# The compressed unit of a prompt's attention: four-pass float32 product, or one float32r product of split operands

## The chip, the cores and the metric

The kernel runs on one core of a Trainium2 chip. The metric is the device time of one execution in microseconds; the median of several runs is compared. Times inside an execution come from one profiled execution, in microseconds (us) from the start of its span. PE is TensorE's stream of matrix products, PEld its loads of weights, DVE VectorE, ACT ScalarE, POOL GpSimd and SP SyncE.

## What is computed

One step of a one-layer decoder trunk, for a prompt of 1024 positions and for eight samples of eight positions: half a SwiGLU, a mixer of attention (8 query heads of 64, 2 key/value heads) and Mamba-2, another half SwiGLU, a last norm. The attention has three branches, whose outputs are weighted by gates and added. The change concerns the first of them, in the prompt: keys and values summarised from blocks of 32 positions at a stride of 16, so 63 rows for 1024 positions. Cut to it, the reference is:

```python
def compress(rows, pe, w1, w2):
    ...   # blocks of 32 rows, stride 16, plus pe
    return jax.nn.silu(blk @ w1) @ w2

def cmp_attention(q, q_pos, kc, vc, slopes):
    ...
    s = jnp.einsum('btghd,bngd->bghtn', qg, kc).astype(jnp.float32) / math.sqrt(HEAD_DIM)
    ...
    p = masked_softmax(s, dist >= 0)
    o = jnp.einsum('bghtn,bngd->btghd', p.astype(vc.dtype), vc)
    return o.reshape(b, Tq, ATT_HEADS, HEAD_DIM), p

o = g[:, :, 0] * o_cmp + g[:, :, 1] * o_sel + g[:, :, 2] * o_win
```

All is float32.

## The kernel before

The kernel goes through its stages in the order of the text: first feed-forward, projections and state-space mixer, keys and values, queries, the prompt's attention, the samples' attention with the output projection, second feed-forward, last norm. Within a stage, and some way across its borders, the order of instructions on each engine is made at build time by a scheduler that works with estimated durations and priorities; on the chip each engine then goes through its own queue in that order, and semaphores hold an instruction until its operands are there.

**Two kinds of products.** Most products of the kernel are done in float32r after a split of each operand into a high part (rounded to float32r, usually by ScalarE) and a low part (the rest, by a subtraction): `split(hi, lo, src, eng)`. The products of probabilities with values are done in plain float32 instead, and show as two records each in the trace.

**Values.** In the stage of keys and values, `cmp_finish(1, ab)` makes the 63 summarised value rows of both groups in one PSUM tile `c2p` (L1523) and copies them into `VAc`, 64 rows by 2 groups by 64 columns, in the pool `kv`, zeroed by GpSimd at L1404 (the 64th row stays zero). `VA` holds the full value rows of the two other branches by blocks of 128 positions. `KA`, the keys, lies behind `VAc` in the pool.

**The prompt's attention** (from L1752) runs over eight tiles of 128 queries in the order 2, 7, 6, 5, 4, 3, 1, 0. Between them it also summarises the samples' cached rows (`compress_sample`: rows gathered into `chk`, products `cA`, L1733 to L1735), so that these products lie in the same stretch of TensorE's queue. For a tile the scores of all heads with the summarised keys are made (`s_cmp`), turned into probabilities `pc` and scaled by the gate. Then for each of the two groups of four heads: scores `s` with the keys of the two other branches (L1808, L1810, masks L1813), their maxima (L1818, L1821, L1822), exponentials `pb` (L1824), scaling by the gate, and a loop over the "units". A unit is one block of 128 key positions, or, as the last one, the 64 compressed rows. For each unit four transposes (L1846) put the probabilities of the four heads side by side into one PSUM tile `pT` (two of them), a copy brings it to `pt` (VectorE or ScalarE in turn), and a product (L1855) of weights `VA` or `VAc` and moving `pt` adds to the PSUM tile `O`. Units go in pairs: an even unit writes rows 0 to 63 of `O`, an odd one rows 64 to 127, issued one behind the other. The number of full units is 2, 4, 6, 8, 10, 11, 12, 13 for tiles 0 to 7; so the compressed unit stands alone but in tiles 5 and 7, where it is the second of a pair. At the end of a group the upper half of `O` is copied to `ob` and added to the lower half into `qT` (L1865, L1866). `O` is one PSUM tile, used by all groups in turn.

Of the functions below, the lines that matter are `VAc` at L1401, L1404 and L1526, and the loop over units from L1838 to L1859.

Of the kernel before, what the change touches and what calls it, by code (L numbers as in the profile page):

```python
# [10 lines left out]
F32 = mybir.dt.float32  # L11
F32R = mybir.dt.float32r
# [6 lines left out]
P = 128  # L19
# [22 lines left out]
def f32(ap):  # L42
    return ap.bitcast(F32)
# [37 lines left out]
def hybrid_step(ctx: ExitStack, tc: tile.TileContext, *aps):  # L81
    nc = tc.nc
# [4 lines left out]
    def pool(name, bufs=1, side="left", space=None, reuse="tile"):  # L87
        kw = {} if space is None else {"space": space}
        if space is None:
            kw["side"] = side  # L90
        return tc.tile_pool(name=name, bufs=bufs, reuse_waits=reuse, **kw)
# [101 lines left out]
    def side(name):  # L193
        return PS.tile([P, 512], F32, name=name, tag="side", bufs=3)
# [71 lines left out]
    def copy(eng, out, src):  # L266
        return nc.scalar.copy(out, src) if eng == "a" else ENGINES[eng].tensor_copy(out, src)  # L267

    def sub(eng, out, x, y, op=OP.subtract):
        ENGINES[eng].tensor_tensor(out, x, y, op=op)  # L270
# [10 lines left out]
    def split(hi, lo, src, eng, heng="a"):  # L281
        copy(heng, hi, src)
        sub(eng, lo, src, f32(hi))
# [380 lines left out]
    K = F1  # L664
# [728 lines left out]
    KV = KVs.enter_context(pool("kv"))  # L1393
# [4 lines left out]
    VA = KV.tile([P, 2, 8, 2, 64], F32, name="VA")  # L1398
    KAc = KV.tile([P, 2, 64], F32R, name="KAc")
    KBc = KV.tile([P, 2, 64], F32R, name="KBc")  # L1400
    VAc = KV.tile([64, 2, 64], F32, name="VAc")  # L1401
    KA = KV.tile([P, 2, 2, TP], F32R, name="KA")
    for t_ in (f32(KAc), f32(KBc), VAc):
        nc.gpsimd.memset(t_, 0.0)  # L1404

    def cmp_hidden(K, ya, yb, kv, m, bufs=1):

        xh = K.tile([P, 2, 2, m + 1], F32, name="cxh", tag="nat", bufs=bufs)
        x_, hs = xh[:, 0], xh[:, 1]
        nc.scalar.activation(x_[:, :, :m], ya, AF.Identity, bias=biask[:, kv:kv + 1])  # L1410
        if yb is not None:
            nc.vector.tensor_tensor(x_[:, :, :m], x_[:, :, :m], yb, op=OP.add)
        nc.scalar.activation(hs[:, :, :m], x_[:, :, :m], AF.Tanh, scale=0.5)
        nc.vector.scalar_tensor_tensor(hs[:, :, :m], hs[:, :, :m], 1.0, x_[:, :, :m], op0=OP.add, op1=OP.mult)
        return hs

    with pool("kvt", bufs=2) as KT, pool("kvtmp", bufs=2) as K:
# [93 lines left out]
        def cmp_finish(kv, ab):  # L1511
            va, vb = (x[:, :P].rearrange("p (g c) -> p g c", g=2) for x in ab)
            hs = cmp_hidden(K, va[:, :, :63], vb[:, :, 1:], kv, 63, 2)
            q = side("c2p")
            if kv == 0:
                kc = q[:64, :126].rearrange("p (g n) -> p g n", g=2)
                nc.tensor.matmul(kc, w2[:, 0], hs[:, :, :63], start=True, stop=True)
                nc.scalar.copy(KAc[0:64, :, :63], kc)
                nc.vector.tensor_copy(KBc[0:64, :, :63], f32(KAc[0:64, :, :63]))
                nc.vector.tensor_tensor(KAc[64:128, :, :63], kc, f32(KAc[0:64, :, :63]), op=OP.subtract)  # L1520
            else:
                for g in range(2):
                    nc.tensor.matmul(q[:63, 64 * g:64 * g + 64], hs[:, g, :63], w2[:, 1],  # L1523
                                     start=True, stop=True)
                vc = q[:63, :P].rearrange("p (g d) -> p g d", g=2)
                nc.vector.tensor_copy(VAc[:63], vc)  # L1526

        def keys(br, kT):
            a = br - 1
# [26 lines left out]
        for c in range(3, 5):  # L1556
            gate(G, hs[:, c - 3], c)
        cmp_finish(0, ab)
        ab = cmp_products(1, *rows_)
        keys(1, k1)  # L1560
# [6 lines left out]
        hs = G.tile([P, 3, 2, P], F32, name="hs", bufs=1)  # L1567
        gate(G, hs[:, 0], 6)
        cmp_finish(1, ab)
        positions(0)  # L1570
        v2 = proj(2, 1)
# [102 lines left out]
    with pool("att", bufs=2) as K, pool("att_ps2", bufs=3, space=PSUM) as PS2, \  # L1674
            pool("att_ps", bufs=1, space=PSUM) as PS1:
        def b1(name):
            tag = "cT" if name == "c2" else name
            return PS1.tile([P, 512], F32, name=name, tag=tag, bufs=2 if name == "pT" else 1)
# [72 lines left out]
        for qi, qt in enumerate(KN["qt"]):  # L1751
# [13 lines left out]
            for h in range(NH):  # L1765
# [5 lines left out]
                             start=False, stop=True, skip_group_check=True)  # L1771
# [13 lines left out]
            for g in range(2):  # L1785
                PT = {}
                for br in range(2):
# [6 lines left out]
                    for hh_ in range(4):  # L1794
                        pb = K.tile([P, 1024 if br == 0 else 640], F32, name=f"pb{br}", bufs=5)
                        pbs.append(pb)
                        st, parts = 0, []
                        for i in range(ns):
# [7 lines left out]
                            if br == 1 and qt >= 4 and st == 0:  # L1806
                                masks.append((0, medge))
                            nc.tensor.matmul(s, QAs[g][:, hh_], KA[:, br, g, kk], start=True, stop=False,  # L1808
                                             skip_group_check=True)
                            nc.tensor.matmul(s, QBq[g][:97, hh_], KB[:97, br, g, kk], start=False, stop=not masks,  # L1810
                                             skip_group_check=True)
                            for j, (c, mk) in enumerate(masks):
                                nc.tensor.matmul(s[:, c:c + P], identb, mk, start=False,  # L1813
                                                 stop=(j == len(masks) - 1), skip_group_check=True)
# [18 lines left out]
                    for hh_ in range(4):  # L1833
                        h, pb = 4 * g + hh_, pbs[hh_]
                        scale(KN["pb"][qi][4 * br + hh_], pb[:, :nk], pb[:, :nk], sm[:, 1 + br, h:h + 1])
                    PT[br] = (pbs, k0, nk // P)
                O = b1("o")
                units = [(VA[:, br, PT[br][1] + i, g], PT[br][0], i, P)  # L1838
                         for br in range(2) for i in range(PT[br][2])]
                units.append((VAc[:, g], None, 0, 64))  # L1840
                held = []
                for ui, (v, pb, i, kn) in enumerate(units):
                    tq_ = b1("pT")
                    for hh_ in range(4):
                        src = pb[hh_][:, P * i:P * i + P] if pb is not None else pc[:, 4 * g + hh_, :]
                        nc.tensor.transpose(tq_[:kn, P * hh_:P * hh_ + P], src, ident)  # L1846

                    pt = K.tile([P, 512], F32, name="pt", bufs=4)
                    c_ = copy("av"[ui % 2], pt[:kn], tq_[:kn])
                    held.append((v, pt[:kn]))  # L1850
                    if ui % 2 or ui == len(units) - 1:

                        with tc.high_priority():
                            for u, (v_, p_) in enumerate(held):
                                mm = nc.tensor.matmul(O[64 * u:64 * u + 64], v_, p_, start=(ui < 2), skip_group_check=True,  # L1855
                                                      stop=(ui - len(held) + 1 + u >= len(units) - 2))
                                if u < len(held) - 1:
                                    tc.add_manual_dep(mm.ins, c_.ins.name, mybir.DependencyInfo(
                                        mybir.DependencyClass.Sync, mybir.DependencyReason.DATA), reason="pair")  # L1859
                        held = []  # L1860
# [470 lines left out]
    for j, m in enumerate(MB[5:] + MB[:5]):  # L2331
# [13 lines left out]
        for i, n in blocks(288):  # L2345
            nc.tensor.matmul(sums[:n, i:i + 1], sq[:, P * i:P * i + n], ones[:, :1], start=(j == 0 and i == 0),
                             stop=(j == KD - 1), skip_group_check=True)
# [185 lines left out]
```

## Time and profile before

| | before |
|---|---|
| runs, us | 2471.36, 2468.21, 2470.27 (median 2470.27) |
| profiled execution, us | 2475.45 |
| its span, us | 2473.8 |
| keys, values, queries | to 1138 us |
| prompt's attention | 1138 to 1550 us |
| samples' attention and output projection | 1550 to about 1760 us |
| TensorE busy, share of the span | 97% |

The shares of busy time on the page are averages over all stages. The windows cut them by stage. The chain of work follows the end of the run, or of a stretch, back through what released each instruction; time on it is time that the end waited for. In a timeline the start of an instruction and that of the next on the same engine give what it holds the engine; a record of TensorE is longer than that, since the ends of its instructions overlap the next ones.

### The profile page before, as it was taken

What the parts mean: (1) busy time and instruction counts of PE and PEld (TensorE: products, weight loads), DVE (VectorE), ACT (ScalarE), POOL (GpSimd) and SP (SyncE); (2) the same over time, 40 slices, a digit from 0 to 9 for tenths busy, and PEclk for the clock granted to TensorE, in tenths of its full rate; (3) what the DMA queues carried; (4) which work ended last, traced back from release to release, by engine and by line L of the source; (5) the groups of instructions that cost most, each with busy time, mean ns of one, the idle gap of its engine ahead of it and who ended that gap; (6) DMA issues with size and microseconds to landing.
All of it is one profiled execution on the core that took longest, in us unless ns stands there. A gap on an engine that the chain in (4) does not pass through costs nothing.

```text
span 2473.8 us, 48193 instructions
## 1 busy us (share of the span) xinstructions
PE 2408.8 (97%) x19026; PEld 2222.8 (90%) x19026; DVE 1744.7 (71%) x3673; ACT 1131.2 (46%) x2501; POOL 418.3 (17%) x533
## 2 busy tenths in 40 slices
PE   7999999999999999999999999999999999999998
PEld 6999999999999998997667766677899999999998
DVE  6777776677778855655656666777967676768776
ACT  7544444441133254425666675444545454543113
POOL 0000000011134343333434343111000000001110
PEclk9999999999999999999999998999999999999999
DMA  4334343598652333423110104476235353559654
GB/s 162 134 133 160 130 164 129 175 338 306 230 190 84 126 116 102 119 69 127 40 64 35 69 35 148 130 250 213 89 123 171 120 174 120 174 213 370 238 209 153
DMA packets 230446, 379.07 MB, mean 153 GB/s; under 512 B 18509, under 2 KB 147705, under 8 KB 228812
## 3 DMA queue, kind: packets, MB, share of 16 engines
q1 hardware_dynamic: 210248, 318.02, 37.7%
q0 software_dynamic: 7600, 38.59, 4.5%
q10 hardware_dynamic: 12372, 19.38, 2.2%
q8 instruction: 150, 2.46, 0.4%
q14 instruction: 76, 0.62, 0.1%
HBM read 255.66 MB, written 124.40 MB: 154 GB/s over the span
## 4 chain that ended last, share of the span: by engine, by line
PE 86%; DVE 6%; DMA 4%; ACT 3%; issue 1%; POOL 0%; ACTq 0%; DVEq 0%; POOLq 0%
PE dq L634 6%; PE gY L367 6%; PE dq L633 6%; PE dq L635 6%; PE gY L368 6%; PE gY L366 6%; PE gX L367 5%; PE gX L366 5%; PE gX L368 5%; PE o L1855 3%; PE pT L1846 3%; PE s L1808 1%; PE xbc L250 1%; PE xbc L251 1%; PE xbc L252 1%; PE cA L1733 1%
## 5 line engine op out<-in xcount | busy, mean ns | idle before, releaser
L634 PE MATMUL dq<-db,da 128*128 128x256 f32 (+1 forms) x1232 | 353.2, 288 | 0.3 <-DVE da L270 0.3
L635 PE MATMUL dq<-db,da 128*128 128x256 f32 (+1 forms) x1232 | 352.8, 288 | 0.0
L633 PE MATMUL dq<-db,da 128*128 128x256 f32 (+1 forms) x1232 | 349.8, 288 | 2.7 <-DVE Cc L386 2.2
L642 DVE TENSOR_TENSOR xT<-xT,dq 128x256 f32<-128x256 f32 (+1 forms) x456 | 186.9, 432 | 84.8 <-PE dq L635 83.2
L270 POOL TENSOR_TENSOR ds<-dw 128x512 f32<-128x512 f32 x22 | 29.5, 1341 | 1228.1 <-DVE wlo L270 508.0
L633 PEld LDWEIGHTS dq<-db,da 128*128 128x128 f32 x1232 | 230.5, 189 | 3.3 <-DVE Cc L386 2.5
L635 PEld LDWEIGHTS dq<-db,da 128*128 128x128 f32 x1232 | 232.8, 189 | 0.0
L634 PEld LDWEIGHTS dq<-db,da 128*128 128x128 f32 x1232 | 231.9, 188 | 0.6 <-DVE da L270 0.5
L267 ACT CAST whi<-ws 128x512 fp32r<-128x512 f32 x156 | 96.5, 623 | 205.9 <-PE gY L368 137.6
L270 DVE TENSOR_TENSOR wlo<-raw,whi 128x512 fp32r<-128x512 f32 x184 | 125.5, 687 | 83.9 <-ACT whi L267 83.5
L267 ACT CAST da<-ds 128x512 fp32r<-128x512 f32 x88 | 52.6, 623 | 234.7 <-PE dq L635 93.4
L267 ACT CAST whi<-raw 128x512 fp32r<-128x512 f32 x181 | 112.4, 626 | 72.0 <-PE g L414 19.5
L270 DVE TENSOR_TENSOR wlo<-ws,whi 128x512 fp32r<-128x512 f32 x156 | 106.7, 687 | 42.4 <-ACT whi L267 41.9
L1824 ACT ACTIVATE pb<-s,mx 128x256 f32<-128x256 f32 (+3 forms) x192 | 105.0, 552 | 59.7 <-DVE mx L1822 37.6
L1846 PEld LDWEIGHTS pT<-ident,pb 128*128 128x128 f32 x528 | 59.6, 143 | 45.8 <-issue 40.1
L1821 DVE TENSOR_REDUCE mx<-s 128x1 f32<-128x384 f32 (+2 forms) x128 | 66.6, 536 | 44.0 <-PE s L1813 34.1
L366 PE MATMUL gY<-B3h,whi 128*128 128x256 f32 (+1 forms) x320 | 91.5, 287 | 1.5 <-ACT whi L267 1.4
L366 PE MATMUL gX<-B6h,whi 128*128 128x256 f32 (+1 forms) x320 | 91.3, 286 | 0.9 <-ACT Cc L373 0.9
L367 PE MATMUL gX<-B6h,wlo 128*128 128x256 f32 (+1 forms) x320 | 91.4, 286 | 0.6 <-DVE wlo L270 0.6
L367 PE MATMUL gY<-B3h,wlo 128*128 128x256 f32 (+1 forms) x320 | 91.6, 287 | 0.2 <-DVE wlo L270 0.2
L277 POOL TENSOR_TENSOR pb<-pb,sm 128x640 f32<-128x640 f32 (+7 forms) x70 | 85.1, 1238 | 37.6 <-DVE sm L1831 34.0
L367 PE MATMUL gY<-B2h,wlo 128*128 128x256 f32 (+1 forms) x320 | 91.4, 286 | 0.0
(763 smaller groups left out, 8548.1 us busy)
## 6 DMA issues: line engine op xcount, KB each, us to landing
db<-GD SPq DMA_DIRECT2D x42, 1632.0 KB
GD<-Cc SPq DMA_DIRECT2D x154, 272.0 KB
GD<-his SPq DMA_DIRECT2D x84, 272.0 KB
raw<-in_ffn_wu_dram SPq DMA_DIRECT2D x22, 1024.0 KB
dw<-in_ffn_wd_dram SPq DMA_DIRECT2D x44, 512.0 KB
raw<-in_ffn_wg_dram SPq DMA_DIRECT2D x21, 1024.0 KB
GD<-hp SPq DMA_DIRECT2D x70, 272.0 KB
db<-GD SPq DMA_DIRECT2D x14, 1088.0 KB
```

Source lines behind the costliest of these rows:

```text
L267: return nc.scalar.copy(out, src) if eng == "a" else ENGINES[eng].tensor_copy(out, src)
L270: ENGINES[eng].tensor_tensor(out, x, y, op=op)
L277: nc.gpsimd.tensor_tensor(out, x, by.to_broadcast(list(x.shape)), op=OP.mult)
L366: nc.tensor.matmul(q, ah[:, k], b_, start=first, stop=False, skip_group_check=True)
L367: nc.tensor.matmul(q, al[:, k], b_, start=False, stop=False, skip_group_check=True)
L368: nc.tensor.matmul(q, ah[:, k], c_, start=False, stop=(k == 3), skip_group_check=True)
L633: nc.tensor.matmul(q, x, bh[:, u, o], start=first, stop=False, skip_group_check=True)
L634: nc.tensor.matmul(q, y, bh[:, u, o], start=False, stop=False, skip_group_check=True)
L635: nc.tensor.matmul(q, x, bl[:, u, o], start=False, stop=(u == np_ - 1), skip_group_check=True)
L642: nc.vector.tensor_tensor(x, x, q, op=OP.subtract if i == 4 else OP.add)
L1824: nc.scalar.activation(pb[:, st:st + pn], s, AF.Exp, bias=mx[:, 0:1], accum_out=part[:, hh_, i:i + 1])
L1846: nc.tensor.transpose(tq_[:kn, P * hh_:P * hh_ + P], src, ident)
```

## The change

`VAc` becomes 128 rows by 2 groups by 128 columns of float32r: the high parts of the values in columns 0 to 63, the low parts in 64 to 127, and the same 64 rows once more in rows 64 to 127 (a copy of rows 0 to 62 to 64 to 126). For the compressed unit the transposed probabilities are split: the high parts go to rows 0 to 63 of a float32r tile `ph`, the low parts to rows 64 to 127. `ph` takes its place among the four buffers of `pt`. One product of 128 rows, 128 columns of weights and 512 moving columns then writes all 128 rows of `O`: rows 0 to 63 get the high values with both parts of the probabilities, rows 64 to 127 the low values with both, and the two halves are added at the end of the group as before. The compressed unit takes no part in the pairs any more. A last full unit with an even number (tiles 5 and 7) is issued alone.

```diff
-    VAc = KV.tile([64, 2, 64], F32, name="VAc")
+    VAc = KV.tile([P, 2, P], F32R, name="VAc")
     KA = KV.tile([P, 2, 2, TP], F32R, name="KA")
-    for t_ in (f32(KAc), f32(KBc), VAc):
+    for t_ in (f32(KAc), f32(KBc), f32(VAc)):
         nc.gpsimd.memset(t_, 0.0)
...
-                nc.vector.tensor_copy(VAc[:63], vc)
+                split(VAc[:63, :, :64], VAc[:63, :, 64:], vc, "v")
+                nc.vector.tensor_copy(VAc[64:127], f32(VAc[:63]))
...
+                    if pb is None:
+                        ph = K.tile([P, 512], F32R, name="ph", tag="pt", bufs=4)
+                        split(ph[:64], ph[64:], tq_[:64], "v")
+                        with tc.high_priority():
+                            nc.tensor.matmul(O, v, ph, start=False, stop=True, skip_group_check=True)
+                        continue
                     pt = K.tile([P, 512], F32, name="pt", bufs=4)
-                    c_ = copy("av"[ui % 2], pt[:kn], tq_[:kn])
-                    held.append((v, pt[:kn]))
-                    if ui % 2 or ui == len(units) - 1:
+                    c_ = copy("av"[ui % 2], pt, tq_)
+                    held.append((v, pt))
+                    if ui % 2 or ui == len(units) - 2:
...
-                                                      stop=(ui - len(held) + 1 + u >= len(units) - 2))
+                                                      stop=False)
```

## Rows read from the trace of the kernel before

**Rows 1.** The page: busy time (us, share, instructions), and its chain by engine.

```profile
PE 2408.8 (97%) x19026; PEld 2222.8 (90%) x19026; DVE 1744.7 (71%) x3673; ACT 1131.2 (46%) x2501; POOL 418.3 (17%) x533
...
PE 86%; DVE 6%; DMA 4%; ACT 3%; issue 1%; POOL 0%; ACTq 0%; DVEq 0%; POOLq 0%
```

**Rows 2.** Windows: us; busy of PE, PEld, DVE, ACT, POOL; granted clock; DMA.

```profile
1060.00:1138.00 78.00, 77.24 (x620) 76.11 (x619) 41.25 (x99) 20.86 (x35) 27.81 (x62) 1.00 0.31 101
1138.00:1550.00 412.00, 398.86 (x2651) 285.98 (x2651) 265.17 (x641) 267.73 (x721) 159.31 (x235) 0.98 0.19 68
```

**Rows 3.** The chain of work from 1138 to 1550 us, shares by line.

```profile
by line: PE o L1855 19.1%; PE pT L1846 15.8%; PE s L1808 7.9%; PE cA L1733 6.9%; PE cA L1735 6.5%; PE s L1810 6.3%; PE cA L1734 6.3%; PE cT L1712 6.3%; DMA chk<-in_cache_cmp_dram,idx 4.8%; PE s L1813 2.2%; ACT pb L1824 1.9%; DVE mx L1821 1.
```

**Rows 4.** Chain (start, us, line), then TensorE's timeline (start, record, instruction).

```profile
1160.21 1.01 PE o L1855 x4
...
1162.31 1.07 PE L1855 MATMUL o<-pt,VAc 64*64 64x512 f32 x2
1163.31 0.66 PE L1846 MATMUL pT<-ident,pb 128*128 128x128 f32 x4
```

**Rows 5.** A mixed pair, tile 7: the chain, then the compressed half in the timeline.

```profile
1220.28 2.00 PE o L1855 x4
...
1221.21 1.07 PE L1855 MATMUL o<-pt,VAc 64*64 64x512 f32 x2
```

**Rows 6.** Timeline of TensorE: four float32r products of scores in a row.

```profile
1172.56 0.48 PE L1808 MATMUL s<-KA,QA 128*128 128x512 f32 x1
1172.87 0.39 PE L1810 MATMUL s<-KB,QB 97*128 97x512 f32 x1
1173.11 0.40 PE L1808 MATMUL s<-KA,QA 128*128 128x512 f32 x1
1173.34 0.40 PE L1810 MATMUL s<-KB,QB 97*128 97x512 f32 x1
```

**Rows 7.** The stage's end: a window, TensorE's timeline, a product from the chain.

```profile
1536.00:1540.00 4.00, 4.00 (x18) 2.27 (x16) 2.99 (x12) 1.84 (x7) 1.76 (x4) 0.50 0.00 2
...
1533.60 0.47 PE L1808 MATMUL s<-KA,QA 128*128 128x128 f32 x1 [0.25 <-ACT pb L1824]
...
1539.99 1.96 PE L1855 MATMUL o<-pt,VAc 64*64 64x512 f32 x2
...
1546.57 1.39 PE L1855 MATMUL o<-pt,VAc 64*64 64x512 f32 x2
...
1556.67 0.43 PE wout L251
```

**Rows 8.** Landings of gathered rows on the chain, and one compressed product's timeline.

```profile
1365.39 10.30 DMA chk<-in_cache_cmp_dram,idx
1453.43 9.67 DMA chk<-in_cache_cmp_dram,idx
...
1366.58 1.07 PE L1855 MATMUL o<-pt,VAc 64*64 64x512 f32 x2
```

**Rows 9.** Groups from 1138 to 1550: count, busy, mean ns, idle before, releasers.

```profile
L1824 ACT ACTIVATE pb<-s,mx 128x256 f32<-128x256 f32 (+3 forms) x192 | 105.0, 552 | 59.7 <-DVE mx L1822 37.6 <-DVE mx L1818 20.4 <-PE pT L1846 1.4
...
L267 DVE COPY pt<-pT 128x512 f32<-128x512 f32 (+1 forms) x68 | 46.8, 689 | 40.9 <-PE pT L1846 40.4
L267 ACT COPY pt<-pT 128x512 f32<-128x512 f32 (+1 forms) x80 | 46.7, 584 | 29.3 <-PE pT L1846 29.1
L1717 DVE TENSOR_TENSOR tl<-cT,th 128x512 fp32r<-128x512 f32 x64 | 44.0, 687 | 16.6 <-ACT th L267 16.1
```

**Rows 10.** Timeline: copies of the compressed unit, first and tightest case, and that product.

```profile
1158.18 0.58 ACT L267 COPY pt<-pT 64x512 f32<-64x512 f32 x1
...
1528.02 0.57 ACT L267 COPY pt<-pT 64x512 f32<-64x512 f32 x1
...
1529.61 1.07 PE L1855 MATMUL o<-pt,VAc 64*64 64x512 f32 x2
```

**Rows 11.** Instructions that write VAc: count, duration ns, start, form.

```profile
L1404 POOL MEMSET VAc<- x1: 198/198/198, 1013.0 to 1013.0; 64x128 f32 x1
L1526 DVE COPY VAc<-c2p x1: 282/282/282, 1077.2 to 1077.2; 63x128 f32<-63x128 f32 x1
```

## What the change should do to the time

> **What bounds the kernel now.** I read the page's busy shares and its chain of work first [rows 1]: TensorE is busy 97% of the span, and 86% of the chain that ended last is TensorE's. A microsecond of TensorE's work is therefore worth about one of the run unless the stage it lies in is limited by something else. The change lies in two places: the making of `VAc` at 1077 us, and the compressed unit of the prompt's attention, sixteen times between 1138 and 1550 us. The table of windows [rows 2] shows that stage: TensorE busy 398.86 of 412 us, so 13.1 us idle; VectorE busy 265, ScalarE 268, GpSimd 159. So VectorE and ScalarE each have about 145 us free there. A busy share is not yet a limit (records overlap, and the profile models their ends), so I read the stage's own chain next [rows 3]: the TensorE lines named in it make 77.3% of the 412 us, the products L1855 alone 19.1%; 4.8% are two landings of the gathered rows, and the rest, at most 18%, holds ScalarE, VectorE and smaller TensorE lines. The stage is mostly TensorE's, not purely.
>
> **The product itself.** In the chain a pair of float32 products of full units takes 1.01 us (four records, two passes each) [rows 4]. The compressed product alone, half as many rows, takes the same: from its start at 1162.31 to that of the next work at 1163.31, 1.00 us (its record lasts 1.07, a drain of 0.07 beyond). A pair is cheap because its halves run in two column halves at once. In four of the sixteen cases (prompt tiles 5 and 7, two groups each) the compressed product is itself the second of a pair. There the rows show no overlap [rows 5]: the two together hold the chain for 2.00 us from 1220.28, and the compressed one starts only at 1221.21. So in all sixteen the compressed unit costs 1.00 us of its own, and splitting the four mixed pairs costs nothing: the full unit keeps its 1.00.
>
> The Trainium skill has a rule for the missing overlap: "TensorEngine Tiling (Array Packing)", section Key Properties, says tiles work independently, but that changing the tiling mode drains the engine. A 128-row and a 64-row tile are two modes, and the 2.00 us of the mixed pair agrees. By the promise of tiles alone, without that sentence, the mixed pair would last 1.01 us, and splitting it would lose four times a new product.
>
> The replacement is one float32r product, 128 rows by 128 columns of weights, 512 moving columns. The same form stands in the scores, L1808 [rows 6]: the first of four in a row holds the engine 0.31 us (1172.56 to the next start at 1172.87), those behind it 0.24 and 0.23 (to 1173.11, to 1173.34). The new product stands alone between other kinds of work, so I take 0.31 and keep 0.23 as the other end. Fourteen products at full clock: 14 x (1.00 - 0.31) = 9.7 us (10.8 with 0.23). The last two are dearer [rows 7]: the granted clock is 0.50 (1.2 GHz) from 1536 to 1540 us, after TensorE had waited for ScalarE at 1533.60, and their records last 1.96 and 1.39 us, so that they hold the engine 1.89 and 1.32. A 512-column float32r product behind that, at 1556.67, takes 0.43, against 0.23 [rows 6]: 1.46 and 0.89 saved, 2.35 together. TensorE's saving: 12.0 us, up to 13.2. Weight loads are also fewer (one record for two); they lie beside earlier products, and I count nothing.
>
> **What of it lies on the path.** Of the two landings on the stage's chain [rows 8] the first lasts from 1365.39 to 1375.69 us and covers one compressed product (1366.58): what is saved there only makes TensorE wait for the landing. That takes 0.7 away: 11.3. The other landing on the chain, 9.67 us from 1453.43, covers none.
>
> **The split of the probabilities.** Before, one copy out of PSUM (12 times ScalarE, 4 times VectorE). After, a ScalarE copy and then a VectorE subtraction that waits for it, 16 of each. The nearest rows [rows 9]: a ScalarE copy takes 0.584 us in the mean and a VectorE copy 0.689; the subtraction `tl` from one PSUM tile, the same form on twice the partitions, 0.687 us. Added work: 4 x 0.58 = 2.3 us on ScalarE, 12 x 0.69 = 8.3 us on VectorE (the other four replace copies of 0.69). Is the product later for it? [rows 10]: the copy ends 3.55 us ahead of the product in the first case, the widest (1158.18 + 0.58 = 1158.76, product at 1162.31 [rows 4]), and 1.02 in the tightest (1528.59, 1529.61); there are sixteen, and the middle one is 2.7. The subtraction and its hand-over, some 0.8 us, fit into every one of them. The cover is the TensorE work that is queued between, scores and transposes of the next group; if it were gone, each case would pay 0.8 us, 12.8 together. What is queued behind the new VectorE instruction are the maxima of the next scores, for which ScalarE's exponentials wait (37.6 us in the stage for L1822 and 20.4 for L1818 [rows 9]). Bounds of the 8.3 us: nothing, where VectorE would have waited anyway, as its copies do (40.4 us for transposes [rows 9]); all 8.3, if each stood in front of such a maximum; added work gains nothing. VectorE's costliest line on the chain has under 2% [rows 3], so I take a tenth, 0.8 us. ScalarE's 2.3 us goes the same way, at a tenth 0.2. The PSUM bank `pT` is held 0.8 us longer; there are two, and the next use of that one is the second unit of the next group, over 3 us later in the first case (1163.31 [rows 4] against a copy that ended at 1158.76): nothing, and at most 0.8 us in a case if that lead went.
>
> **Making VAc.** One VectorE copy (0.28 us) becomes a ScalarE copy, a VectorE subtraction and a VectorE copy into the upper rows; the memset on GpSimd, 0.198 us, covers four times the words [rows 11]. I take 0.3 + 0.3 + 0.4 us, in front of a first use 85 us later (1077.17 against 1162.31), in a window where TensorE is busy 77.24 of 78 us [rows 2]: nothing; if something behind it on VectorE were late, under 1 us. The memset lies 149 us ahead of that use, on an engine that is free for most of the span [rows 1]: nothing, at most three times its row, 0.6, if it were waited for. `VAc` takes 512 bytes more per partition, and `KA` behind it moves up by that; no wait hangs on it.
>
> **The sum.** 11.3 - 0.8 - 0.2 = 10.3 us if TensorE's time is all that counts. At most 22.7% of the stage's chain is not in the named TensorE lines, and those parts (exponentials after maxima, landings) do not shrink when TensorE does: 22.7% of 10.3 is 2.3, given back as waits. Forecast: 8 us less. The profiled execution took 2475.45 us (span 2473.8), which is 5.2 above the median of the runs, 2470.27; 2467.4 on its scale is 2462.3 on that of the runs. One more unknown is that the order of instructions on each queue is planned at build time from estimated durations, so that other durations give another order for the whole stage. The trace of before cannot show the new one; it is a reason for the width, not a term.
>
> **Rivals.** (1) The gain is absorbed: TensorE ends each product sooner and then waits for ScalarE's exponentials or the landings, because these set the pace. For: ScalarE's waits for maxima are 58 us in the stage [rows 9], and a landing of 10.3 us stands on its chain [rows 8]. Against: 77% of the chain is TensorE's. Three quarters of 10.3 lost leaves 2.6: 2467.7. Chance 0.17. (2) The low clock spreads: granted clock falls after waits [rows 7], and less work makes more waits. One more stretch like that from 1536 to the product at 1546.57, 10.6 us that would have taken half, costs 5.3 us: -8 + 5.3, 2467.6. Chance 0.05. The Trainium skill, "TensorE: Matmul & The Clock Gate", section Why this matters for your kernels, warns against idle gaps between bursts for the same reason; the rows at 1536 us agree. (3) Slower: the split is late. The subtraction queues on VectorE behind maxima and scalings; with a lag of L behind the ScalarE copy, the product stalls by L + 0.69 - 2.7 us in the middle case, and TensorE, being in order, with it. It becomes a loss over 4.9 us when the stalls exceed 12.9, 0.8 per case, L above 2.8 us: four queued instructions of 0.69. At L = 3, 16 x 0.99 = 15.8 - 8 = +7.8: 2478. For it: VectorE is busy 64% of the stage, and 12 instructions are added. Against: leads of 2.7 us and a third of its time free. Chance 0.10. (4) The product does not run as the scores do but in several passes: then 1.00 stays and only the added 1.0 us of VectorE and ScalarE counts: 2471. The scores have operands of the same type, so 0.03.
>
> **How the numbers follow.** Forecast, 2457 to 2465.3: 0.65; (1) to (4) as said. What a measurement of this kernel can tell from no change is about 0.2%, 4.9 us. Faster: the forecast, and the upper end of (1): 0.68. Same: most of (1), (2), (4): 0.22. Slower: (3): 0.10. Range: 2457 (all 13.2 us) to 2472; above lie most of (3), and below a stage that also loses its stretch of low clock, some 0.05.
>
> **What would show it.** Right: 16 records of L1855's compressed product with 128 columns of weights and some 0.23 to 0.32 us to the next start; the split's subtraction ended before its product could start; the stage from 1138 us shorter by about 8 us, and the stages behind it unchanged in length. Wrong: waits of TensorE on the subtraction in front of these products (3), a sum of idle time above 13 us by as much as the products lost (1), more slices below full clock (2). If the stage is not shorter by the products' saving but others are, the plan of the order has moved more than the change itself.

## The result

The changed kernel takes 2484.46 us, the kernel before 2472.11 in the same comparison: a ratio of 1.0051, 95% interval 1.0039 to 1.0064. It is slower by 12.4 us, where 8 us less had been forecast. The profiled execution took 2485.05 us, its span 2483.3.

The page of the changed kernel, busy time and chain by engine, answers to [rows 1]:

```profile
PE 2406.9 (97%) x19010; PEld 2226.1 (90%) x19010; DVE 1756.2 (71%) x3686; ACT 1135.9 (46%) x2506; POOL 417.4 (17%) x533
...
PE 85%; DVE 6%; DMA 3%; ACT 3%; issue 1%; POOL 0%; ACTq 0%; SPq 0%; DVEq 0%; POOLq 0%
```

Its windows, with the columns of [rows 2], and one behind them:

```profile
1060.00:1138.00 78.00, 77.24 (x621) 76.12 (x619) 41.04 (x100) 19.73 (x35) 27.97 (x62) 1.00 0.31 101
1138.00:1550.00 412.00, 388.99 (x2614) 284.86 (x2613) 273.49 (x638) 270.54 (x720) 157.20 (x233) 0.97 0.15 57
1550.00:1560.00 10.00, 8.32 (x29) 4.37 (x29) 5.64 (x24) 4.49 (x9) 2.15 (x3) 0.50 1.06 397
```

Up to 1138 us nothing has moved. Between 1138 and 1550 us TensorE is busy 9.9 us less than before, and idle 23.0 us instead of 13.1; and at 1550 the stage isn't over. The last compressed product starts at 1555.19 us, against 1546.57 [rows 7], so the stage has become 8.6 us longer although its largest engine has less to do. That is most of the 9.5 us between the two spans (2483.3 and 2473.8); behind that product both kernels take 928 us to the end.

The new product does what was forecast. Its forms in the changed kernel (count, shortest, middle and longest record in ns), and its first case in TensorE's timeline:

```profile
L267 ACT CAST ph<-pT x16: 567/579/582, 1162.0 to 1551.8; 64x512 fp32r<-64x512 f32 x16
L270 DVE TENSOR_TENSOR ph<-pT,ph x16: 683/685/686, 1162.6 to 1553.2; 64x512 fp32r<-64x512 f32 x16
...
L1853 PE MATMUL o<-ph,VAc x16: 391/477/796, 1166.8 to 1555.2; 128*128 128x512 f32 x16
```

```profile
1166.77 0.48 PE L1853 MATMUL o<-ph,VAc 128*128 128x512 f32 x1
1167.09 0.38 PE L1847 MATMUL pT<-ident,pb 128*128 128x128 f32 x2
```

One record instead of two, and 0.32 us from its start to that of the next work, against 1.00 [rows 4]. So the loss is not in the product. Two other things are new in the trace.

**The exponential's table is loaded late.** The table load of ScalarE stands behind a wait for VectorE of 9 us, and the stage's first exponential waits for the load. The changed kernel's ScalarE:

```profile
1129.79 1.05 ACT L1657 CAST w1h<-raw 128x1024 fp32r<-128x1024 f32 x1 [1.12 <-DMA raw<-in_cmp_w_v_dram]
1139.83 1.28 ACT L1825 ACT_TABLE_LOAD   x1 [8.99 <-DVE mx L1819]
1141.13 0.58 ACT L1825 ACTIVATE pb<-s,mx 128x384 f32<-128x384 f32 x1
```

**The order of the stage is another one.** All through the stage the queues of TensorE, VectorE, ScalarE and GpSimd hold the same instructions in another order. The last gather of a sample's rows, issued at 1453.43 us before [rows 8], is issued at 1473.11 now; the samples' summaries run later against the prompt's tiles.

### The profile page after: what moved, and what is told of

Read it like the earlier page. It is cut to its first block, busy times and chain, and to the rows that moved or that the text cites. A ratio compares the mean times of both kernels' runs of the same rounds, so it can differ in the third digit from the quotient of the medians.

```text
span 2483.3 us, 48163 instructions
## 1 busy us (share of the span) xinstructions
PE 2406.9 (97%) x19010; PEld 2226.1 (90%) x19010; DVE 1756.2 (71%) x3686; ACT 1135.9 (46%) x2506; POOL 417.4 (17%) x533
## 4 chain that ended last, share of the span: by engine, by line
PE 85%; DVE 6%; DMA 3%; ACT 3%; issue 1%; POOL 0%; ACTq 0%; SPq 0%; DVEq 0%; POOLq 0%
PE dq L633 6%; PE dq L634 6%; PE dq L635 6%; PE gY L367 6%; PE gY L368 6%; PE gY L366 6%; PE gX L367 5%; PE gX L366 5%; PE gX L368 5%; PE pT L1847 3%; PE o L1862 2%; PE s L1809 1%; PE xbc L250 1%; PE xbc L251 1%; PE xbc L252 1%
## 5 line engine op out<-in xcount | busy, mean ns | idle before, releaser
L270 POOL TENSOR_TENSOR ds<-dw 128x512 f32<-128x512 f32 x22 | 29.1, 1320 | 1231.5 <-DVE wlo L270 512.2
L1847 PE MATMUL pT<-ident,pb 128*128 128x128 f32 x528 | 89.3, 286 | 9.6 <-ACT pt L267 3.3
L367 PE MATMUL gX<-B7h,wlo 128*128 128x256 f32 (+1 forms) x320 | 91.4, 286 | 0.3 <-DVE wlo L270 0.3
```

The source lines that it names most:

```text
L367: nc.tensor.matmul(q, al[:, k], b_, start=False, stop=False, skip_group_check=True)
```

## The experiments

Theory 1: the saving is real and the newly planned order lost it. Theory 2: the split lost it. To hold the order, every instruction was tied to the next one on its engine in a prescribed sequence; instructions with no counterpart in the other kernel (ScalarE's high copies in tiles 5 and 7, VectorE's subtractions in the other tiles) were left to the scheduler. Each run was compared with the kernel before on its own chip, so ratios are what to compare; the medians of before were 2471.0 to 2472.0 us.

### The order held: four combinations

```diff
         hybrid_step(tc, *args)
+        _pin(tc)    # ties each instruction to the next one of a stored order, engine by engine
```

The control, the kernel before in its own order:

> The kernel before with an explicit chain between each instruction and the next on its engine, in the order that it has anyway: nothing else is changed. It is the control for the two runs with foreign orders. Both theories (the order made the loss; the split made the loss) expect the time of before within 0.2%, 2467 to 2476 us. If it moves by more, the chain itself costs something, and the two other runs are read against this one.

Measured: 2470.67 us, ratio 0.9998 (0.9987 to 1.0010). The chain costs nothing that the runs can tell.

> The changed kernel, all of its instructions, but issued on every engine in the order of before (each split stands where the copy stood, the new product where the old one stood). Theory 1 (the saving is real and the newly planned order of the attention stage lost it): TensorE's own time falls by the 10.6 us that the two traces show for it and little is given back, so about 2461 us, between 2457 and 2465. Theory 2 (the split itself, its extra work on ScalarE and VectorE and its hand-over, lost it): no better than before, 2471 to 2485 us.

Measured: 2471.86 us, ratio 1.0001 (0.9988 to 1.0014). Held in the old order the change loses nothing, but it also gains nothing, to within some 3 us: theory 1 had 2461 us, and fails in that half.

> The kernel before, float32 product and plain copies, but issued on every engine in the order that the changed kernel has (a plain copy stands where the split's first half, or on VectorE its second half, stood). Theory 1: the order's cost without the saving, 2484 + 10 = about 2494 us, at least 2485. Theory 2: the time of before, 2468 to 2476 us, since none of the split is there.

Measured: 2491.30 us, ratio 1.0075 (1.0062 to 1.0088), with nothing of the split in it. This is theory 1's half that holds. With the old products the new order costs 19.6 us, with the new ones 12.6 (2484.46 against 2471.86); in the new order the change's own work saves 6.8 us by the medians (2491.30 to 2484.46; 5.9 by the ratios, whose intervals just touch), in the old order none.

### Another order, nothing else

```diff
-                    if ui % 2 or ui == len(units) - 1:
+                    if ui % 2 or ui >= len(units) - 2:
```

> The kernel before, planned freely, with one line changed: in the two prompt tiles (four units) where the compressed unit's product was issued as a pair with the last full block's, the two are issued apart. Same instructions, same sizes, none of the change. A pair that mixed 64 and 128 rows held TensorE 2.00 us, and two single ones hold 1.00 us each, so by that work nothing changes: theory 2 expects the time of before within 2 us. Theory 1: the planner makes another order of the stage, and the time moves by 3 us or more, to either side, up to some 15.

Measured: 2471.50 us, ratio 1.0003 (0.9993 to 1.0013). This answers two questions. The split of the mixed pairs costs nothing, as the prediction had it from [rows 5]. And a new order as such needn't cost: this edit makes one as well, at no price. It is a smaller one: when the two sequences of TensorE's records are matched, about 540 records of the stage stand elsewhere than in the trace of before, in the changed kernel about 1600. It is the particular order that costs.

### Why nothing is gained in the old order

TensorE's waits by line in 1138 to 1550 us (in total, times, longest), first the control, then the change in the old order:

```profile
PE s L1808 <- ACT pb L1824: 3.2, 8, 0.7
...
PE pT L1846 <- ACT pt L267: 1.0, 2, 0.6
...
PE pT L1846 <- DVE pt L267: 0.8, 2, 0.4
```

```profile
PE s L1809 <- ACT pb L1825: 6.1, 11, 1.2
PE pT L1847 <- DVE pt L267: 3.1, 3, 1.7
...
PE pT L1847 <- ACT pt L267: 1.6, 3, 0.6
```

Scores wait 2.9 us more for ScalarE's exponentials, transposes 2.9 us more for the copies that free their PSUM tile. Three candidates for the rest: the split's extra work (S), a lower clock and the late table (C), or cover by other engines (A).

High parts only, in the old order:

```diff
-                        split(ph[:64], ph[64:], tq_[:64], "v")
+                        copy("av"[ui % 2], ph[:64], tq_[:64])
...
-                            nc.tensor.matmul(O, v, ph, start=False, stop=True, skip_group_check=True)
+                            nc.tensor.matmul(O, v[:64], ph[:64], start=False, stop=True, skip_group_check=True)
```

> The changed kernel in the order of before, without the low parts: one copy of the transposed probabilities to float32r on the engine that made it before, no subtraction, and one float32r product of 64 rows with the high part of the values' rows (the low parts of probabilities and values are left out of the output's compressed unit). TensorE's products are as short as the change's and the split's second step is gone. Theory S (the split's extra work and its hand-over ate the saving in the old order): 2460 to 2465 us. Theory C (the shorter products are answered by more low clock, and what is left goes to the late load of the exponential's table): as the change in the old order, 2469 to 2473 us, with a mean clock near 0.987. Theory A (TensorE's saved time was covered by other engines anyway): 2470 to 2473 us with the clock unchanged and longer waits.

Measured: 2467.91 us, ratio 0.9987 (0.9977 to 0.9997), between S and C. By the ratios 3.5 us less than the whole change, with intervals that still overlap: the split's second step looks like a part of the answer, not all.

The long product on the split operands, in the old order:

```diff
-                            nc.tensor.matmul(O, v, ph, start=False, stop=True, skip_group_check=True)
+                            nc.tensor.matmul(O, f32(v), f32(ph), start=False, stop=True, skip_group_check=True)
```

> The changed kernel in the order of before, with the product read as float32 again: 128 rows, 128 columns, 512 moving columns, in several passes, 1.00 us of TensorE for each instead of 0.25 to 0.31. The split is all there. Against the change in the old order (2471.9 us, clock 0.987): theory S says that the split costs the 10 us, so the old product on top gives about 2480 us; theory C says that 10.6 us of work come back, and with them about 10 us less at the low clock, about 5 us: 2475 to 2478 us at a mean clock of 0.988 or more; theory A says that nothing changes, 2471 to 2473 us.

Measured: 2470.79 us, ratio 0.9997 (0.9985 to 1.0009). From the start of a product to that of the second instruction behind it, summed over the sixteen, the timelines give 16.7 us here and 7.5 with the short product: 9.3 us of TensorE's work more, and no time more, to within some 4 us. That is A's time. But the clock did not stay where A puts it. The windows from 1138 to 1550 us of the control, the change in the old order, and this kernel:

```profile
1138.00:1550.00 412.00, 398.51 (x2680) 285.87 (x2679) 271.62 (x663) 273.53 (x732) 160.00 (x235) 0.99 0.19 69
```

```profile
1138.00:1550.00 412.00, 393.19 (x2659) 291.72 (x2659) 275.42 (x662) 273.83 (x729) 159.95 (x237) 0.97 0.19 68
```

```profile
1138.00:1550.00 412.00, 395.71 (x2681) 290.27 (x2680) 275.43 (x662) 272.58 (x729) 159.54 (x237) 0.99 0.19 69
```

Granted clock 0.99, 0.97, 0.99. Over all runs of these kernels the mean clock of the whole span is 0.9887, 0.9866 and 0.9883. A thousandth of it is 2 x 0.001 x 2470 = 4.9 us at half speed, at most 2.5 us of time; from run to run of one kernel it goes with 1 to 2 us (1.4 in the control). So the 0.0021 between the control and the change in the old order are worth 2 to 5 us, an estimate. The last two kernels differ in the product alone: 0.0017 of it goes with the short product, with an uncertainty of 0.0016, so that the fall of the clock is only just clear of the spread of the runs. One place shows it, 14 us long, first with the short product, then with the long one at the same point of the work:

```profile
1397.50:1401.50 4.00, 4.00 (x26) 2.86 (x24) 2.89 (x6) 1.56 (x4) 0.00 (x0) 1.00 0.00 0
1401.50:1405.50 4.00, 2.64 (x19) 1.73 (x18) 3.77 (x15) 3.26 (x11) 2.15 (x4) 1.00 0.02 4
1405.50:1409.00 3.50, 3.48 (x16) 3.18 (x17) 1.42 (x4) 2.70 (x8) 3.38 (x5) 0.52 0.00 0
```

```profile
1402.50:1406.50 4.00, 4.00 (x21) 2.42 (x21) 3.34 (x8) 1.11 (x2) 0.00 (x0) 1.00 0.01 4
1406.50:1410.00 3.50, 2.39 (x19) 1.70 (x18) 2.88 (x12) 2.71 (x9) 1.64 (x3) 1.00 0.00 0
1410.00:1414.00 4.00, 3.74 (x31) 3.32 (x31) 2.40 (x5) 3.66 (x12) 3.88 (x4) 1.00 0.00 0
```

In both TensorE pauses over a microsecond right behind the compressed product, mostly for exponentials. In the first its clock then falls to 1.2 GHz, in the second it doesn't. What decides between the two is not shown here.

### The late table

```diff
-    VAc = KV.tile([64, 2, 64], F32, name="VAc")
+    VAc = KV.tile([P, 2, P], F32, name="VAc")      # used in its old part only
```

> The kernel before with one change: the tile of the values' compressed rows is allocated as 128 rows of 2x128 (as in the changed kernel) and used in its old part only. TensorE's order is that of before. Theory 3 (the larger tile moves what is allocated behind it, so that the first exponential waits for two engines, and the load of its table stands behind the first of the two waits): the table load is found on the chain at the stage's start, 1.3 us, and the low clock that follows it at most another 2 to 3 us: 2472.5 to 2476 us. Without it: before, 2470 to 2473 us.

Measured: 2475.42 us, ratio 1.0011 (1.0000 to 1.0022): 2.7 us by the ratio, 4.4 by the medians. TensorE's order is that of before, the split isn't there, and the load is late. ScalarE in the control, then in this kernel:

```profile
1129.40 1.28 ACT L1824 ACT_TABLE_LOAD   x1
1138.81 0.58 ACT L1824 ACTIVATE pb<-s,mx 128x384 f32<-128x384 f32 x1 [8.13 <-DVE mx L1818]
```

```profile
1138.39 1.28 ACT L1824 ACT_TABLE_LOAD   x1 [9.32 <-DVE mx L1818]
1139.69 0.58 ACT L1824 ACTIVATE pb<-s,mx 128x384 f32<-128x384 f32 x1
```

The first exponential now waits for VectorE and for GpSimd, where it waited for VectorE alone; in the trace the wait for VectorE has become an instruction of its own, and the table load, which belongs to the exponential, stands behind it. The only difference between the two kernels is the tile's size, so it is what moved in memory behind the tile. The other way round, an early load in the changed kernel, old order:

```diff
             sm = K.tile([P, 3, NH], F32, name="sm")
+            if qi == 0:
+                nc.scalar.activation(sm[:1, 0, :1], ident[:1, :1], AF.Exp)
```

> The changed kernel in the order of before, with one exponential of a single element ahead of the first one of the stage on ScalarE, so that the table is loaded while ScalarE still waits. Theory 3: 1.3 us of the load and what it does to the clock come back against the change in the old order (2471.9 us): 2468 to 2470.5 us. If the start of the stage is not where it is lost: 2471 to 2473 us.

Measured: 2468.73 us, ratio 0.9986 (0.9975 to 0.9997). The load is at 1129.23 us again. This is a whole kernel, faster than both: by about 3 us than before, by 16 than the changed one. Either run by itself puts the late table near what two such comparisons can tell; they agree, in opposite directions, on some 3 us.

The Trainium skill, "ScalarE: Activation LUTs", section What ACT_TABLE_LOAD costs, gives 1283 ns for the load and 1380 more for a drain. The trace has the first (1.28 us) and not the second: the exponential starts 0.02 us behind the load, in the changed kernel and in the widened one.

Both side effects away at once, high parts only and the early load:

> The old order, high parts only (the low parts of probabilities and values are left out of the compressed unit), and the early table load. Against the change in the old order the two apart were worth 4.0 us (no subtraction and no low copy) and 3.1 us (early table). If they add: 2464 to 2466 us, near the 2462 us of the forecast, and the forecast's saving is there when both side effects are gone. If they don't add, because what is late next is late in both: 2467 to 2469 us.

Measured: 2465.59 us, ratio 0.9978 (0.9969 to 0.9986), as expected if they add, and together clear of the change in the old order. So 5.4 us of the forecast's 8 are there, in the old order and without the two side effects; its mean clock is 0.9871, against 0.9887 of the control, worth another 2 to 4 us by the same estimate. One wait of TensorE shows how the two hang together: at the stage's start its transposes wait for a copy by VectorE, 1.73 us with the change in the old order. With the wider tile alone that wait is 1.68 us, with the early table alone 1.73; it is gone in the control and in this kernel, where both side effects are away.

> The changed kernel in its own new order, with one exponential of a single element ahead of ScalarE's first exponential of the stage, so that the table is loaded while it waits. In the old order this was worth 3.1 us. If the late table is a cost of its own, beside the order: 2480 to 2482 us against 2484.5; if the start's delay is lost in later waits: 2483 to 2486 us.

Measured: 2482.67 us, ratio 1.0050 (1.0036 to 1.0065) against 1.0051 of the changed kernel as it is. In the new order the early load brings nothing that can be told; the time lost there has other causes.

### Where the new order loses

The changed kernel, its order cut in two at 1468 us of the trace of before, both ways:

> The changed kernel; all that before issues ahead of the compressed product of tile 4's second group (1468 us of its trace) in the new order, the rest (the last sample's summaries, tiles 3, 1 and 0) in the old one. Whole new order: 2484.5 us; whole old order: 2471.9. Theory L (the new order costs by its end: the last sample's summaries come late, and tile 0 and the sample queries' loads with them): 2472 to 2476 us. Theory D (it costs all along, by small waits and a lower clock): two thirds of the loss stay, 2479 to 2483 us.

Measured: 2492.10 us, ratio 1.0084 (1.0067 to 1.0101), more than the whole new order. Its trace shows why it tells little: the summaries that the new order had put off are caught up with ahead of the cut, and TensorE is idle 10.4 us in the group before it.

> The changed kernel, cut at the same place the other way: the old order ahead of it, the new one for the last sample's summaries, tiles 3, 1 and 0 and all behind them. Theory L: most of the loss of 12.6 us is here, 2480 to 2484 us. Theory D: a third or less, 2472 to 2476 us.

Measured: 2475.77 us, ratio 1.0022 (1.0010 to 1.0034). About 4 of 12.6 us lie behind 1468 us. Theory L, the late end, falls as the main cause; a third or less is what theory D had. Three more cuts of this kind, the old order first:

> The changed kernel, old order up to the first score of the attention stage, new order behind. Theory D (the cost is spread over the stage): all of the 12.6 us is there, 2482 to 2486 us. Theory P (the cost arises ahead of the stage, where the order differs too): 2472 to 2478 us.

> The changed kernel, old order up to the compressed product of tile 7's second group (1255 us of the trace of before, 29% of the stage), new order behind. Theory D: about 2480 to 2483 us, on a line from 2484.5 down to the 2475.8 us measured for the cut at 81% of the stage. One place ahead of the cut: 2475 to 2478 us; one place behind it: 2483 to 2486 us.

> The same with the cut at tile 5's first group (1367 us, 56% of the stage). Theory D: about 2477.5 to 2480.5 us. One place ahead of the cut: 2475 to 2477 us; one place between 56% and 81%: 2482 us or more.

| new order from | us | ratio, 95% interval |
|---|---|---|
| stage's start (1138 us) | 2483.25 | 1.0056 (1.0039 to 1.0073) |
| tile 7, second group (1255) | 2489.54 | 1.0066 (1.0049 to 1.0082) |
| tile 5, first group (1367) | 2488.65 | 1.0070 (1.0056 to 1.0084) |
| tile 4, second group (1468) | 2475.77 | 1.0022 (1.0010 to 1.0034) |

With the new order from the stage's start all of the loss is there, so theory P falls. The time of the cut at 1255 us fits no theory; that of the cut at 1367 us fits one by its number only (2482 or more, one place between 56% and 81% of the stage). Neither can place the loss: both took about 5 us more than the whole new order, so a cut there has a cost of its own. The trace of the cut at 1367 shows it: two us behind the cut TensorE waits 3.30 us for an exponential, as it does in neither whole order, and its clock is 0.78 in the 23 us from there.

```profile
1369.13 0.69 PE L1809 MATMUL s<-KA,QA 128*128 128x384 f32 x1 [3.30 <-ACT pb L1825]
...
1367.00:1390.00 23.00, 19.54 (x103) 14.61 (x103) 10.99 (x28) 9.70 (x29) 7.84 (x11) 0.78 0.14 61
```

The cut at 1255 has two such waits right behind it, 1.53 and 1.41 us. So where the new order loses is read from whole traces. A first place is in tile 6, ahead of the cuts at 1367 and 1468 us. From 1290 to 1320 us in the changed kernel, then in the change in the old order:

```profile
1290.00:1320.00 30.00, 28.37 (x190) 21.57 (x188) 17.12 (x43) 19.05 (x51) 12.52 (x17) 0.94 0.11 45
```

```profile
1290.00:1320.00 30.00, 29.93 (x216) 22.96 (x215) 18.66 (x45) 20.87 (x57) 11.70 (x17) 1.00 0.00 1
```

In the changed kernel a copy of a sample's gathered rows holds ScalarE up, the exponentials stand behind it, TensorE waits for one of them, and from 1300.5 to 1304 us its clock is 0.51:

```profile
1294.28 0.41 ACT L267 COPY chp<-chk 128x256 f32<-128x256 f32 x1 [2.31 <-DMA chk<-in_cache_cmp_dram,idx]
...
1298.14 0.44 PE L1809 MATMUL s<-KA,QA 128*128 128x384 f32 x1 [1.59 <-ACT pb L1825]
...
1300.50:1304.00 3.50, 3.50 (x18) 3.01 (x17) 1.55 (x4) 1.61 (x5) 3.38 (x4) 0.51 0.00 0
```

A second place is in tiles 5 and 4. That stretch in the changed kernel, then in the change in the old order:

```profile
1367.00:1470.00 103.00, 97.85 (x687) 73.13 (x686) 68.10 (x154) 69.17 (x182) 36.39 (x58) 1.00 0.11 42
```

```profile
1367.00:1470.00 103.00, 101.22 (x705) 76.74 (x705) 70.39 (x166) 71.01 (x192) 41.01 (x64) 0.98 0.16 62
```

TensorE is idle 5.2 us instead of 1.8. Its longest wait there, in the changed kernel, with what ScalarE does meanwhile:

```profile
1435.50 0.39 PE L1847 MATMUL pT<-ident,pb 128*128 128x128 f32 x2
1438.17 0.66 PE L1847 MATMUL pT<-ident,pb 128*128 128x128 f32 x4 [2.28 <-ACT pt L267]
```

```profile
1433.39 0.20 ACT L1825 ACTIVATION_READ_ACCUMULATOR pb<-s,mx 128x1 f32 x1
1435.51 0.40 ACT L267 COPY chp<-chk 128x256 f32<-128x256 f32 x1 [1.92 <-DMA chk<-in_cache_cmp_dram,idx]
1435.82 0.47 ACT L1410 ACTIVATE cxh<-cA,biask 128x254 f32<-128x254 f32 x1
1436.32 0.75 ACT L267 COPY ob<-o 64x256 f32<-64x256 f32 x2
1437.09 0.41 ACT L1413 ACTIVATE cxh<-cxh 128x254 f32<-128x254 f32 x1
1437.53 0.59 ACT L267 COPY pt<-pT 128x512 f32<-128x512 f32 x1
```

ScalarE stands 1.92 us at the copy of a sample's gathered rows, which haven't landed. Behind it in ScalarE's queue stand the copy of `O` and a copy of `pT` that TensorE's next transposes need. That is the kind of place in which this order loses: an instruction that waits for a transfer, put ahead of work that TensorE waits for. ScalarE waits at such copies in the old order too (4.5 us in all with the change, 8.0 in the new order); what stands behind them differs. A third place is the end, where TensorE waits for a scaling by VectorE:

```profile
1550.48 0.45 PE L1847 MATMUL pT<-ident,pb 128*128 128x128 f32 x1 [2.86 <-DVE pb L279]
```

These waits recur. Every run of the changed kernel that has the new order at the place has them: 1.6 us in tile 6 (five runs), 2.0 to 2.3 in tile 4 (six), 2.5 to 2.9 at the end (six); none that has the old order there has them. So the loss is spread over at least three places, as theory D had it in kind. The old products in the new order show only the first of the three above a microsecond (1.35 us), and how their 19.6 us are made up stays open. In the stretch from 1367 to 1470 us the clock is the higher one in the changed kernel (1.00 against 0.98); over whole runs it is the lower one, 0.9838 against 0.9866 with the change in the old order, by the estimate above 3 to 7 us of the 12.6.

## Why the prediction was wrong

**The step that failed is the one that was put outside the sum:** "another order for the whole stage ... a reason for the width, not a term." That term is +12.6 us with the change's work and +19.6 with the old work, as much as TensorE's whole saving or more; the range's upper end, 2472, left it 1.7 us above the median of before. The last sentence of what would show it, that "the plan of the order has moved more than the change itself", is what happened, though not by its sign: no other stage became shorter, the stage itself became longer. Its sign could not be had from the trace of before; that it had a size could have been said by bounds.

**The product: right.** 0.32 us of hold against 0.31 taken; one record of 128 columns; the mixed pairs cost nothing to split. Held in the old order, the sixteen products with the instruction behind each take 7.5 us of TensorE's timeline, in the control 19.2: 11.8 saved, where 12.0 had been forecast.

**The path: wrong in size.** Taking 2.3 us as given back assumed that the parts of the chain that aren't TensorE's stay as they are when TensorE ends earlier. In the old order all 8 us went. The long product on the same split operands shows that 9.3 us of TensorE's work in this stage were free to within some 4 us: the other engines' side effects lay under them, and the clock was higher with them. Rival (1), absorbed, came nearest to that result (2467.7 us, 2.6 less than before) but put it to waits alone; rival (2), the low clock, had the other part (5.3 us) at a chance of 0.05. Here both acted at once, by estimate on 2 to 5 us of clock and the rest waits.

**The split: too small, and not late.** One us was taken for its work on VectorE and ScalarE; without its second step the time is 3.5 us lower by the ratios with the late table and 2.0 with the early one, each within its own uncertainty. But rival (3) did not happen: TensorE's waits on `ph` itself sum to 0.2 us in the changed kernel. The two tables of waits point to where the work costs: at exponentials and copies queued behind it, not at the product that it feeds.

**Making VAc: wrong.** "No wait hangs on it" was said of the bytes that move `KA`. The operations were free, as taken. The bytes gave ScalarE's first exponential a second wait and put 1.28 us of table load on the path, some 3 us in all in the old order. Nothing in the trace of before shows this; the rows of after show it at first sight.

**The sum, with what was measured:** -8 forecast; +8 in the old order (about 3 table, 2 to 3.5 split, the rest clock and waits, of which only table and split together are clear of the uncertainty); +12.6 order. 12.6 us above before by the medians of the combinations, 12.4 in the direct comparison.

What stays open: why the scheduler's order for the changed kernel is the poorer one, and which of its moves carries how much. The cuts show that some 4 us lie behind 1468 us; the others don't take the loss apart, since each cut also makes a sequence that neither kernel has. The new order inside the tiles with the summaries in their old places wasn't tried.

## What to carry to other kernels

Where a build-time scheduler orders the queues, an edit is two changes, the work and a new order; hold the order fixed to measure the first, and give the second a term of its own, of either sign, as large as the largest difference seen between two orders of that stage. Saving on the engine that is busy 97% pays only as far as the others can follow: look for what becomes late next, and for what the pauses do to the clock. After any edit that changes a tile's size, look at the first instruction of each stage for waits that it didn't have.

## What was not expected of the hardware

- 9.3 us of TensorE's work more in a stage of 412 us cost nothing that the runs can tell (2470.79 against 2471.86 us), with the granted clock higher in its presence (0.9883 against 0.9866, just clear of the spread).
- The clock fell to 1.2 GHz behind pauses that were short and broken: 2.64 us busy in 4.00, no single wait over 0.75 us. In tile 6 of the changed kernel it fell behind one wait of 1.59 us. The Trainium skill, "TensorE: Matmul & The Clock Gate", section A second HAM failure mode: psum-queue depth-cycling, tells of such small pauses between groups that make the clock go up and down; the rows at 1401.5 and 1405.5 us agree, and the place with the long product, paused as much without a fall, shows that the pause alone doesn't decide it.
- A table load stands behind its activation's separate wait instruction, so a second wait in front of an activation exposed 1.28 us here that was hidden with one wait.
